# A residual encoder block on one core: the first weight chunk packed with x^T, three staggered chunks, later border transposes, and the last column quarter apart

## The chip, the cores and the metric

The kernel runs on one NeuronCore of one Trainium2 chip. The metric is the device time of one execution in microseconds (us); the runs shown are the median of three with the lowest and the highest. Engines are named as the profile names them: PE is TensorE (PEld its weight loads), DVE is VectorE, ACT is ScalarE, POOL is GpSimd and SP is SyncE, which here only issues DMAs.

## The reference

One layer on x of 256 tokens by 1024 features, all in float32 (D_FF = 2816):

```python
h = rmsnorm(x, ffn1_pre_g);  x = x + 0.5 * rmsnorm(swiglu(h, ffn1_w_in, ffn1_w_down), ffn1_post_g)
h = rmsnorm(x, mix_pre_g)
q_a, f_a, i_a, g_a, q_b, k_b, v_b, f_b, gates = split(h @ w_in)
o_a = rmsnorm(hgrn2_chunkwise(q_a, f_a, i_a), hg_norm_g) * silu(g_a)      # gated linear recurrence
o_b = fox_attention(q_b, k_b, v_b, f_b + fox_f_bias)                      # causal attention with decay
g = sigmoid(gates + b_gate)
y = g[:, 0] * (o_a @ w_branch_a) + g[:, 1] * (o_b @ w_branch_b)
x = x + rmsnorm(y @ w_out, mix_post_g)
x = x + rmsnorm(mem_cross_attention(rmsnorm(x), rmsnorm(mem), w_mq, w_mkv, w_mo), mem_post_g)
h = rmsnorm(x, ffn2_pre_g);  x = x + 0.5 * rmsnorm(swiglu(h, ffn2_w_in, ffn2_w_down), ffn2_post_g)
```

where swiglu(h) is (silu(gate) * up) @ w_down and rmsnorm divides by the root mean square of a row.

## The kernel before

**Arithmetic.** Each float32 product is made of three matmuls. An operand is split into a rounded part ("hi", made by ACT as a cast) and the remainder ("lo" or "lT", made by DVE as a subtraction), and PE adds hi·hi, hi·lo and lo·hi. Weights come in units of 128 x 1024 (512 KB). `unit` (L113) loads one into a buffer `raw` (4 of these), casts it to `hi` (L122, ACT) and makes `lo` (L123, DVE); there are 8 buffers each of `hi` and `lo`, so a further unit can be split only when PE has used up an older one. Activations are kept transposed, features on the partitions, in a `Pair` of hi and lo tiles with 8 blocks (kb) of 128 features. `proj_tok` multiplies one half of the tokens (h = 0 or 1, 128 each) by a chunk of four units: 24 matmuls of 512 columns, kb 0 to 7 in order.

**The head.** L397 to L411. x^T comes over the ACT queue in five DMAs, unit 0 over the SP queue in two halves and units 1 to 3 whole. PE makes 14 warm-up passes on a tile of ones (`WARM` = 7 matmuls). For each kb, `gain_split` (L242) writes hi = x·gain (L247 on ACT, for the very first block L245 on DVE) and the remainder (L248, DVE). `act_first` (L320) then does chunk 0 and chunk 1 of the first feed-forward for both halves: 2 x 48 matmuls into the four `acc` banks.

**A feed-forward.** `ffn` (L288) takes 11 chunks of 256 hidden columns. `act_tok` multiplies, `act_evac` (L306) applies Silu (L308, ACT) and the product (L310, DVE), `flush` (L294) transposes the result and splits it, and `down` (L333) adds the chunk's part of the output into `accs[h][n]`, one PSUM bank for each half h and each 512 columns n. The `down` of the last `STAG` = 4 chunks is kept to the end: first all of half 0, then all of half 1.

**A border.** When half 0 of a stage is summed, `post` (L272) makes the sandwich norm: Square with a row sum on ACT (`ssq`, L219), the product with the gain row on DVE (L279), an inverse root from small DVE operations on 128 x 1 (`rstd_of`, L200: a bit trick, then three Newton steps of two operations), and x += on DVE (L283). `half` (L426) then transposes the new x (`to_T`, L250: 8 transposes of 128 x 128 on PE, L256, into two PSUM banks, then 8 `gain_split`s) and takes the row sums of x. PE meanwhile works on half 1. `after(i)` (L83) places such work behind the i-th matmul from a mark: the constants `L_F1`, `L_IA`, `L_WO`, `L_MK`, `L_MO` say how many matmuls into the next piece of work the transposes come. The program's own scheduler orders each engine's instructions under these limits; the order is fixed when the program is built. There are three such borders: A, from the first feed-forward to the mixer's `i_a` projection; B, from `w_out` to the memory attention; C, from `mo` (the memory attention's output projection, 48 matmuls for half 0, then 48 for half 1) to the second feed-forward.

**The end.** `post(accs[1], 1, grow, 0.5, True)` (L393) makes the last half's norm, and two stores of 256 KB on the SP queue end the program.

Of the kernel before, what the change touches and what calls it, by code (L numbers as in the profile page):

```python
# [16 lines left out]
P = 128  # L17
# [5 lines left out]
NFF = D_FF // FC  # L23
EPS = 1e-6
BIG = 1e30
# [18 lines left out]

WARM = 7

X_AT = 6

# [16 lines left out]
@with_exitstack  # L65
def block_kernel(ctx: ExitStack, tc: tile.TileContext, wts, x_in, xT_in, mem_in, memT_in, cols, rows, fbias, masks, out):
    nc = tc.nc
# [44 lines left out]

    def unit(name, i, parts=1):  # L113
        u = _AT[name] + i
        if u not in cache:
            raw = wp.tile([P, D], F32, tag="raw", name=nm("raw"), bufs=4)
            hi = wp.tile([P, D], F32R, tag="hi", name=nm("hi"), bufs=8)
            lo = wp.tile([P, D], F32R, tag="lo", name=nm("lo"), bufs=8)
            for a in range(0, D, D // parts):
                cut = slice(a, a + D // parts)  # L120
                loads.append(nc.sync.dma_start(raw[:, cut], wts[u][:, cut]).ins)
                S.copy(hi[:, cut], raw[:, cut])  # L122
                V.tensor_tensor(out=lo[:, cut], in0=raw[:, cut], in1=hi[:, cut].bitcast(F32), op=ALU.subtract)  # L123
            cache[u] = (hi, lo)
        return cache[u]
# [74 lines left out]
    def rstd_of(s, scaled=True):  # L200

        v = s1(name="v")
        V.tensor_scalar(out=v, in0=s[:, 0:1], scalar1=s[:, 1:2], scalar2=D * EPS, op0=ALU.add, op1=ALU.add)
        y = s1(name="y")
        V.tensor_scalar(out=y.bitcast(I32), in0=v.bitcast(I32), scalar1=-0.5, scalar2=1597463007.0, op0=ALU.mult, op1=ALU.add)
        for c in (3.0, 12.0, 768.0):
            t = s1(name="t")
            V.scalar_tensor_tensor(out=t, in0=v, scalar=y, in1=y, op0=ALU.mult, op1=ALU.mult)  # L208
            y2 = s1(name="y")
            V.scalar_tensor_tensor(out=y2, in0=t, scalar=c, in1=y, op0=ALU.subtract, op1=ALU.mult)  # L210
            y = y2
        if not scaled:
            return y
        r = s1(name="rstd")
        V.tensor_scalar(out=r, in0=y, scalar1=-1.0 / 256.0, scalar2=None, op0=ALU.mult)
        return r
# [54 lines left out]

    def post(ps, h, grow, factor=1.0, last=False):  # L272

        s = s1(2, name="ss2")
        ts = []
        for j in range(2):
            ssq(s[:, j : j + 1], ps[j])
            t = sp.tile([P, 512], F32, tag="z2", name=nm("post"), bufs=3)
            V.scalar_tensor_tensor(out=t, in0=ps[j], scalar=-factor / 256.0, in1=grow[:, j * 512 : (j + 1) * 512], op0=ALU.mult, op1=ALU.mult)  # L279
            ts.append(t)  # L280
        r = rstd_of(s, scaled=False)
        for j, (t, xh) in enumerate(zip(ts, x_halves(h))):
            V.scalar_tensor_tensor(out=xh, in0=t, scalar=r, in1=xh, op0=ALU.mult, op1=ALU.add)  # L283
            if last:
                nc.sync.dma_start(out[h * P : (h + 1) * P, j * 512 : (j + 1) * 512], xh)


    def ffn(w_in, w_dn, X, r2, n_tok, i_row, first_half, second_half=None):  # L288
# [17 lines left out]
        def act_evac(ps, c, h):  # L306
            sg = sp.tile([P, FC], F32, tag="c1", name=nm("sg"), bufs=7)
            S.activation(sg, ps[:, :FC], AF.Silu, scale=r2[h])  # L308
            a = sp.tile([P, FC], F32, tag="c1", name=nm("at"), bufs=7)
# [22 lines left out]

        def down(c, h):  # L333
            act = acts[c]
            hs = slice(h * P, (h + 1) * P)
            for j in range(2):
                wh, wl = unit(w_dn, 2 * c + j)
                ah, al = act[:, 0, j, hs], act[:, 1, j, hs]
                for n in range(2):
                    ns = slice(n * 512, (n + 1) * 512)  # L340
                    for i, (a, w) in enumerate(((ah, wh), (ah, wl), (al, wh))):
                        MM(accs[h][n], a, w[:, ns], start=(c == 0 and j == 0 and i == 0), stop=(c == NFF - 1 and j == 1 and i == 2))

# [20 lines left out]
        for c in range(n_tok, NFF):  # L364
# [10 lines left out]
            while done < min(c - 1, NFF - STAG):  # L375
# [3 lines left out]
                flush(n + L_ACT)  # L379
                done += 1  # L380
        m = len(log)
# [5 lines left out]
        for c in range(NFF - STAG, NFF):  # L387
            down(c, 1)
        if first_half:
            first_half(m)  # L390
# [13 lines left out]
    S.activation(warm, ones[:, 0:1], AF.Silu)  # L404
    wps = trp()
    for _ in range(WARM):
        MM(wps[:, :P], ones, ones, start=True, stop=True)
    for j in range(4):
        unit("f1_in", j, 2 if j == 0 else 1)
        for i in range(2):  # L410
            gain_split(X1, 2 * j + i, xT[j][:, i, :T], xT[j][:, i, T:], first=2 * j + i == 0)  # L411

# [340 lines left out]
    def gates(c):  # L753
        u = chunk("gates", c)
        z = m4([P, 2, 512], n="zg")
        brow = sp.tile([P, 512], F32, tag="brow", name=nm("brow"), bufs=2)
        nc.sync.dma_start(brow, rows[4 + c // 2, c % 2 * 512 : c % 2 * 512 + 512].partition_broadcast(P))
        for h in range(2):
# [58 lines left out]

    def rows_proj(ps, X, name, h, kbs):
        a, b = h * P, h * P + P
        for kb in kbs:  # L820
            wh, wl = unit(name, kb)
            for n in range(2):
                ns = slice(n * 512, (n + 1) * 512)
# [22 lines left out]
    for c in range(2):  # L846
        u = chunk("mk", c)
        KM.more()
        for j in range(2):
# [97 lines left out]
def _layout(inputs):  # L947
# [41 lines left out]
    def col(v):  # L989
# [11 lines left out]
        [((s == t) if m == 0 else ((s // m) % 2 == 0) & (t // m == s // m + 1)).astype(np.int32) for m in LEVELS], axis=1  # L1001
    )
    r = {
        "wts": wts, "x": nat(a["x"]), "xT": np.concatenate([tra(a["x"]), col(a["ffn1_pre_g"][0])[:, :, None]], axis=2), "mem": nat(a["mem"]), "memT": tra(a["mem"]),
        "cols": cols, "rows": rows, "fbias": a["fox_f_bias"][0].reshape(8, 1), "masks": masks,
# [18 lines left out]
```

## Time and profile before

| what | value |
|---|---|
| runs shown | 808.42 us median of 3 (807.83 to 810.88) |
| the profiled execution | 807.36 us, of which the profile's span is 805.6 us |
| granted TensorE clock, mean | 0.997 |
| weight DMAs, SP queue | 260 whole units of 512 KB, 4.3 us from issue to landing (median) |
| GpSimd | 9.2 us busy |

The page gives the busy time of each engine and its costliest groups. Groups that a view prints by line look like "line engine operation out<-in shapes xcount | busy, mean ns of one | idle before, and what ended it". A timeline row is "start, length, engine, line, operation, tiles, count", with the idle time before it and what ended it in square brackets; rows of like instructions are merged, and the count says how many. Two matmuls of 512 columns start 0.227 us apart though each is shown with 0.39 us, since they are pipelined. The chain of waits follows the work that ended last back to the start.

### The profile page before, as it was taken

The page shows a single profiled execution, that of the slowest core. Times are in us where ns is not written, and L with a number is a line of the kernel's source. Part 1 is how long each engine was busy: PE and PEld are TensorE (multiplying, and loading weights), DVE is VectorE, ACT ScalarE, POOL GpSimd, SP SyncE. Part 2 cuts the span into 40 slices and gives each one's busy share as a digit, 9 for nine tenths or more (in the row PEclk, how much of TensorE's full clock was granted, in tenths as well). Part 3 has the DMA queues.
Part 4 walks back from the last instruction along what each step waited for, and adds up shares of the span by engine and source line. Part 5 has one row for each costly group of instructions (what it writes and reads, how often), then busy time and mean ns, then how long its engine had stood idle before and what let it go on. Part 6 is the DMA issues. An engine that isn't in the chain of part 4 may idle for free.

```text
span 805.6 us, 12769 instructions
## 1 busy us (share of the span) xinstructions
PE 792.6 (98%) x5040; PEld 679.4 (84%) x5040; DVE 525.1 (65%) x837; ACT 414.3 (51%) x623; POOL 9.2 (1%) x20
## 2 busy tenths in 40 slices
PE   8999999999999999999999999999999999999996
PEld 6888888888899889998888888999887788888884
DVE  6865545548776897678675666975659655545544
ACT  6754444537754435447674445645647654434531
POOL 0000000000000100200000000000000000000000
PEclk9999999999999999999999999999999999999998
DMA  8866654555455463643486555455425656665521
GB/s 331 302 223 209 211 200 157 193 173 183 164 203 171 171 195 123 212 155 120 139 291 235 177 161 201 146 197 196 151 77 186 210 185 206 209 201 166 182 79 52
DMA packets 41867, 147.90 MB, mean 184 GB/s; under 512 B 4808, under 2 KB 5200, under 8 KB 41808
## 3 DMA queue, kind: packets, MB, share of 16 engines
q1 hardware_dynamic: 40624, 144.46, 53.2%
q0 software_dynamic: 464, 1.58, 0.6%
q10 hardware_dynamic: 720, 1.05, 0.4%
q8 instruction: 39, 0.64, 0.3%
q14 instruction: 20, 0.16, 0.1%
HBM read 146.02 MB, written 1.06 MB: 183 GB/s over the span
## 4 chain that ended last, share of the span: by engine, by line
PE 89%; DVE 4%; DMA 2%; issue 2%; ACT 1%; SPq 0%; DVEq 0%; ACTq 0%
PE mm L80 63%; PE acc L80 23%; DMA raw<-in_wts_dram 2%; DVE lo L123 2%; PE tr L303 1%; PE tr L80 1%; ACT junk L219 1%; DVE xs L283 1%; PE tr L256 1%; DVE t L208 1%; DVE y L210 0%; ACT hi L122 0%; PE tr L712 0%; DVE post L279 0%; PE tr L901 0%
## 5 line engine op out<-in xcount | busy, mean ns | idle before, releaser
L123 DVE TENSOR_TENSOR lo<-raw,hi 128x1024 fp32r<-128x1024 f32 (+1 forms) x262 | 317.7, 1222 | 93.3 <-ACT hi L122 83.7
L122 ACT CAST hi<-raw 128x1024 fp32r<-128x1024 f32 (+1 forms) x262 | 270.8, 1047 | 140.0 <-PE mm L80 105.1
L80 PE MATMUL mm<-lo,hT 128*128 128x512 f32 x576 | 225.9, 392 | 0.0
L80 PE MATMUL mm<-hi,hT 128*128 128x512 f32 x576 | 225.6, 392 | 0.0
L80 PE MATMUL mm<-hi,lT 128*128 128x512 f32 x576 | 225.1, 391 | 0.1
L80 PEld LDWEIGHTS mm<-hi,lT 128*128 128x128 f32 x576 | 108.2, 188 | 23.0 <-DVE lT L248 0.8
L80 PEld LDWEIGHTS mm<-hi,hT 128*128 128x128 f32 x576 | 108.2, 188 | 22.6 <-ACT hT L247 0.5
L80 PEld LDWEIGHTS mm<-lo,hT 128*128 128x128 f32 x576 | 108.2, 188 | 21.7
L80 PE MATMUL acc<-hi,act 128*128 128x512 f32 x352 | 111.8, 391 | 0.0
L80 PE MATMUL mm<-hT,lo 128*128 128x256 f32 x392 | 111.3, 284 | 0.0
L80 PE MATMUL mm<-hT,hi 128*128 128x256 f32 x392 | 111.2, 284 | 0.0
L80 PE MATMUL mm<-lT,hi 128*128 128x256 f32 x392 | 111.1, 283 | 0.0
L80 PEld LDWEIGHTS acc<-hi,act 128*128 128x128 f32 x352 | 66.1, 188 | 13.4
L80 PEld LDWEIGHTS mm<-lT,hi 128*128 128x128 f32 x392 | 75.2, 192 | 0.1
L80 PEld LDWEIGHTS mm<-hT,hi 128*128 128x128 f32 x392 | 75.2, 192 | 0.1
L80 PEld LDWEIGHTS mm<-hT,lo 128*128 128x128 f32 x392 | 75.2, 192 | 0.1
L80 PE MATMUL acc<-lo,act 128*128 128x512 f32 x176 | 70.0, 398 | 0.0
L308 ACT ACTIVATE sg<-mm,rstd 128x256 f32<-128x256 f32 x40 | 19.0, 474 | 76.2 <-PE mm L80 76.2
L310 DVE SCALAR_TENSOR_TENSOR at<-mm,rstd,sg 128x256 f32<-128x256 f32 x40 | 19.2, 480 | 58.8 <-ACT sg L308 58.8
L80 PEld LDWEIGHTS acc<-lo,act 128*128 128x128 f32 x176 | 33.1, 188 | 6.4
L80 PE MATMUL acc<-hi,hT 128*128 128x512 f32 x96 | 35.5, 396 | 1.6 <-ACT hi L122 1.1
L80 PE MATMUL acc<-hi,lT 128*128 128x512 f32 x96 | 35.4, 396 | 0.5 <-DVE lT L248 0.5
(175 smaller groups left out, 630.2 us busy)
## 6 DMA issues: line engine op xcount, KB each, us to landing
raw<-in_wts_dram SPq DMA_DIRECT2D x260, 512.0 KB, 4.3
grow<-in_rows_dram SPq DMA_DIRECT2D x4, 512.0 KB, 5.8
brow<-in_rows_dram SPq DMA_DIRECT2D x4, 256.0 KB, 4.9
xs<-in_x_dram SPq DMA_DIRECT2D x2, 512.0 KB, 5.5
cbm<-cd POOLq DMA_DIRECT2D x2, 512.0 KB, 8.5
memT<-in_memT_dram SPq DMA_DIRECT2D x2, 512.0 KB, 7.5
ms<-in_mem_dram SPq DMA_DIRECT2D x2, 512.0 KB, 7.8
out_dram<-xs SPq DMA_DIRECT2D x4, 256.0 KB, 2.1
```

What stands on the lines that cost most here:

```text
L80: log.append(PE.matmul(*args, **kw).ins)
L122: S.copy(hi[:, cut], raw[:, cut])
L123: V.tensor_tensor(out=lo[:, cut], in0=raw[:, cut], in1=hi[:, cut].bitcast(F32), op=ALU.subtract)
L208: V.scalar_tensor_tensor(out=t, in0=v, scalar=y, in1=y, op0=ALU.mult, op1=ALU.mult)
L219: S.activation(junk[:, : src.shape[-1]], src, AF.Square, accum_out=dst)
L256: PE.transpose(ps[:, j * P : (j + 1) * P], src(kb), ident)
L283: V.scalar_tensor_tensor(out=xh, in0=t, scalar=r, in1=xh, op0=ALU.mult, op1=ALU.add)
L303: PE.transpose(trv[:, j, h * P : (h + 1) * P], ats[c, h][:, j * P : (j + 1) * P], ident)
L308: S.activation(sg, ps[:, :FC], AF.Silu, scale=r2[h])
L310: V.scalar_tensor_tensor(out=a, in0=ps[:, FC:], scalar=r2[h], in1=sg, op0=ALU.mult, op1=ALU.mult)
```

## The change

The diff below is cut; the new numeric constants `SC_RSTD`, 16.0 and 40/3 only carry scale factors of the new polynomial.

- **Head.** The host packs, for each kb, x^T's block, the matching 512 columns of chunk 0's weights and the gains into one row of 776 floats. Eight DMAs on the SP queue bring them; x^T's own five DMAs on the ACT queue and units 0 to 3 disappear. `X_AT`, the weight load behind which x itself is fetched, goes from 6 to 10, `WARM` from 7 to 8. The gate rows (`brow`) are held behind the latest weight load.
- **Staggered chunks.** `STAG` goes from 4 to 3. For half 0, and for half 1 of the second feed-forward, the kept `down`s go through the left 512 columns of all three chunks before the right 512.
- **Borders.** `L_F1` 18 to 24, `L_IA` 22 to 36, `L_WO` 18 to 12 and `L_MK` 46 to 84 with both transposes of border B moved into the `mk` projection, `L_MO` 18 to 21. `mo` does kb 0 to 2 for both halves first, then kb 3 to 7 of half 0 (left, then right columns), then kb 3 to 7 of half 1.
- **Inverse root.** Two Newton steps are replaced by one and a fourth-order step: five operations where there were six.
- **The end.** The last chunk's right columns of half 1 are done as two quarters of 256, and `post_last` treats left, third and fourth quarter apart, takes the root with Sqrt on ACT, and stores in three parts on two queues. A Sqrt on a dummy behind the last Silu precedes it.

```diff
-STAG = 4
-L_ACT = 15
-L_F1 = 18
-L_IA = 22
-L_WO = 18
-L_MK = 46
-L_MO = 18
+STAG = 3
+L_ACT = 21
+L_F1 = 24
+L_IA = 36
+L_WO = 12
+L_MK = 84
+L_MO = 21
-WARM = 7
-X_AT = 6
+WARM = 8
+X_AT = 10
...
+    def parts_of():
+        return [wp.tile([P, D], F32R, tag=t, name=nm(t), bufs=8) for t in ("hi", "lo")]
...
-        for c in (3.0, 12.0, 768.0):
-            t = s1(name="t")
-            V.scalar_tensor_tensor(out=t, in0=v, scalar=y, in1=y, op0=ALU.mult, op1=ALU.mult)
-            y2 = s1(name="y")
-            V.scalar_tensor_tensor(out=y2, in0=t, scalar=c, in1=y, op0=ALU.subtract, op1=ALU.mult)
-            y = y2
+        V.scalar_tensor_tensor(out=t, in0=v, scalar=y, in1=y, op0=ALU.mult, op1=ALU.mult)
+        V.scalar_tensor_tensor(out=z, in0=t, scalar=3.0, in1=y, op0=ALU.subtract, op1=ALU.mult)
+        V.scalar_tensor_tensor(out=t, in0=v, scalar=z, in1=z, op0=ALU.mult, op1=ALU.mult)
+        V.scalar_tensor_tensor(out=w, in0=t, scalar=40.0 / 3.0, in1=t, op0=ALU.subtract, op1=ALU.mult)
+        V.scalar_tensor_tensor(out=y, in0=w, scalar=80.0, in1=z, op0=ALU.add, op1=ALU.mult)
...
+    def post_last(ps, h, grow, factor):
+        cuts = [(0, 0, 512), (1, 0, 256), (1, 256, 512)]
+        for i, (j, a, b) in enumerate(cuts):
+            ssq(s[:, i : i + 1], ps[j][:, a:b])
+            if i == 1:
+                V.tensor_scalar(out=sums, in0=s[:, 0:1], scalar1=s[:, 1:2], scalar2=D * EPS, op0=ALU.add, op1=ALU.add)
+            if i == 2:
+                S.activation(y, s[:, 2:3], AF.Sqrt, bias=sums)
+                V.tensor_tensor(out=v, in0=s[:, 2:3], in1=sums, op=ALU.add)
+            V.scalar_tensor_tensor(out=t, in0=ps[j][:, a:b], scalar=scaled, in1=grow[:, j * 512 + a : j * 512 + b], op0=ALU.mult, op1=ALU.mult)
+        V.reciprocal(z, y)
+        V.scalar_tensor_tensor(out=t, in0=v, scalar=z, in1=z, op0=ALU.mult, op1=ALU.mult)
+        V.scalar_tensor_tensor(out=r, in0=t, scalar=3.0, in1=z, op0=ALU.subtract, op1=ALU.mult)
+        for t, (j, a, b), eng in zip(ts, cuts, (nc.sync, nc.scalar, nc.sync)):
+            V.scalar_tensor_tensor(out=xh, in0=t, scalar=r, in1=xh, op0=ALU.mult, op1=ALU.add)
+            eng.dma_start(out[h * P : (h + 1) * P, j * 512 + a : j * 512 + b], xh)
...
+            if c == NFF - 1 and h == 1 and not first_half:
+                with tc.issue_after(silu.ins):
+                    S.activation(warm, ones[:, 0:1], AF.Sqrt)
...
-        for c in range(NFF - STAG, NFF):
-            down(c, 0)
+        for cut in (left, right):
+            for c in range(NFF - STAG, NFF):
+                down(c, 0, (cut,))
...
-            post(accs[1], 1, grow, 0.5, True)
+            for cut in (left, right):
+                for c in range(NFF - STAG, NFF):
+                    if (c, cut) != (NFF - 1, right):
+                        down(c, 1, (cut,))
+            for cut in ((512, 768), (768, 1024)):
+                down(NFF - 1, 1, (cut,))
+            post_last(accs[1], 1, grow, 0.5)
...
-    xT = [m4([P, 2, T + 1], n="xT") for _ in range(KB // 2)]
-    for kb in range(2):
-        S.dma_start(xT[0][:, kb], xT_in[:, kb])
-    for j in range(1, 4):
-        S.dma_start(xT[j], xT_in[:, 2 * j : 2 * j + 2])
+    heads = [m4([P, T + 512 + KB], n="head") for _ in range(KB)]
+    for kb in range(KB):
+        loads.append(nc.sync.dma_start(heads[kb], head_in[kb]).ins)
...
+    for kb in range(KB):
+        if kb % 2 == 0:
+            cache[_AT["f1_in"] + kb // 2] = parts_of()
+        hi, lo = (p[:, kb % 2 * 512 : kb % 2 * 512 + 512] for p in cache[_AT["f1_in"] + kb // 2])
+        w = heads[kb][:, T : T + 512]
+        S.copy(hi, w)
+        gain_split(X1, kb, heads[kb][:, :T], heads[kb][:, T + 512 + kb : T + 512 + kb + 1], first=kb == 0)
+        V.tensor_tensor(out=lo, in0=w, in1=hi.bitcast(F32), op=ALU.subtract)
...
-    half(X3, r3, 0, G_MEM, m + L_WO)
...
-        if c == 0:
-            half(X3, r3, 1, G_MEM, m + L_MK)
+            if c == 0:
+                half(X3, r3, j, G_MEM, m + (L_WO, L_MK)[j])
...
-    for h in range(2):
-        m = len(log)
-        rows_proj(po[h], AO, "mo", h, range(0, 4))
-        rows_proj(po[h], AO, "mo", h, range(4, 8))
-        if h == 1:
-            half(X4, r4, 0, G_F2, m + L_MO)
-        post(po[h], h, g3)
+    for kb in range(3):
+        for h in range(2):
+            rows_proj(po[h], AO, "mo", h, (kb,))
+    for n in range(2):
+        rows_proj(po[0], AO, "mo", 0, range(3, KB), (n,))
+    post(po[0], 0, g3)
+    m = len(log)
+    rows_proj(po[1], AO, "mo", 1, range(3, KB))
+    half(X4, r4, 0, G_F2, m + L_MO)
+    post(po[1], 1, g3)
```

More of the change, by code (lines that the diff above doesn't have):

```diff
@@ L116, in unit @@
             raw = wp.tile([P, D], F32, tag="raw", name=nm("raw"), bufs=4)
[L117 to L123, printed above, removed]
+            hi, lo = parts_of()
+            loads.append(nc.sync.dma_start(raw, wts[u - 4]).ins)
+            S.copy(hi, raw)
+            V.tensor_tensor(out=lo, in0=raw, in1=hi.bitcast(F32), op=ALU.subtract)
             cache[u] = (hi, lo)
@@ L270, in load_row, with post @@
         return r
-    def post(ps, h, grow, factor=1.0, last=False):
+    def post(ps, h, grow, factor=1.0, store=False):
         s = s1(2, name="ss2")
@@ L338, in down @@
                 ah, al = act[:, 0, j, hs], act[:, 1, j, hs]
[L339 to L340 removed]
+                for lo, up in cols:
                     for i, (a, w) in enumerate(((ah, wh), (ah, wl), (al, wh))):
[L342 removed]
+                        MM(accs[h][lo // 512][:, lo % 512 : lo % 512 + up - lo], a, w[:, lo:up], start=(c == 0 and j == 0 and i == 0), stop=(c == NFF - 1 and j == 1 and i == 2 and up % 512 == 0))
         for c in range(n_tok):
@@ L386, in ffn @@
         m = len(log)
-        for c in range(NFF - STAG, NFF):
-            down(c, 1)
         if first_half:
+            for c in range(NFF - STAG, NFF):
+                down(c, 1)
             first_half(m)
@@ L756, in gates @@
         brow = sp.tile([P, 512], F32, tag="brow", name=nm("brow"), bufs=2)
-        nc.sync.dma_start(brow, rows[4 + c // 2, c % 2 * 512 : c % 2 * 512 + 512].partition_broadcast(P))
+        with tc.issue_after(loads[-1]):
+            nc.sync.dma_start(brow, rows[4 + c // 2, c % 2 * 512 : c % 2 * 512 + 512].partition_broadcast(P))
         for h in range(2):
@@ L821, in rows_proj @@
             wh, wl = unit(name, kb)
-            for n in range(2):
+            for n in cols:
                 ns = slice(n * 512, (n + 1) * 512)
@@ L1002, in _layout @@
     )
+    xT = tra(a["x"])
+    gain = col(a["ffn1_pre_g"][0])
+    head = np.stack(
+        [np.concatenate([xT[:, kb], wts[kb // 2][:, kb % 2 * 512 : kb % 2 * 512 + 512], gain], axis=1) for kb in range(KB)]
+    )
     r = {
-        "wts": wts, "x": nat(a["x"]), "xT": np.concatenate([tra(a["x"]), col(a["ffn1_pre_g"][0])[:, :, None]], axis=2), "mem": nat(a["mem"]), "memT": tra(a["mem"]),
+        "wts": wts[4:], "head": head, "x": nat(a["x"]), "mem": nat(a["mem"]), "memT": tra(a["mem"]),
         "cols": cols, "rows": rows, "fbias": a["fox_f_bias"][0].reshape(8, 1), "masks": masks,
```

40 lines of the change are left out of this document (28 added, 12 removed).

## The prediction

> **What bounds the kernel now.** I read the page first, then the chain of waits, then the timeline at the places where the chain leaves PE.
>
> ```profile
> span 805.6 us, 12769 instructions
> PE 792.6 (98%) x5040; PEld 679.4 (84%) x5040; DVE 525.1 (65%) x837; ACT 414.3 (51%) x623; POOL 9.2 (1%) x20
> PE 89%; DVE 4%; DMA 2%; issue 2%; ACT 1%; SPq 0%; DVEq 0%; ACTq 0%
> 10.73 19.03 PE acc L80 x82
> 47.53 10.88 PE mm L80 x48
> 516.46 13.55 PE mm L80 x113
> ```
>
> PE sets the time. The change removes no matmul, so it can move only the stretches without PE: the head, the borders and the tail. A 512-column matmul costs 10.88/48 = 0.227 us, a 256-column one 13.55/113 = 0.12.
>
> **Head.** The timeline of the first 8 us, and two stretches of the windows view (length, busy time and count of PE, PEld, DVE, ACT, POOL, clock, DMA share, GB/s), with one row of the DMA issues:
>
> ```profile
> 3.43 1.28 ACT L404 ACT_TABLE_LOAD   x1 [3.43 <-issue]
> 4.68 0.35 DVE L245 TENSOR_SCALAR hT<-xT 128x256 fp32r<-128x256 f32 x1 [3.66 <-DMA xT<-in_xT_dram]
> 4.73 0.20 ACT L404 ACTIVATE warm<-ones 128x1 f32<-128x1 f32 x1
> 4.84 0.60 ACT L122 CAST hi<-raw 128x512 fp32r<-128x512 f32 x1
> 5.07 0.48 DVE L248 SCALAR_TENSOR_TENSOR lT<-xT,hT 128x256 fp32r<-128x256 f32 x1
> 5.47 0.69 DVE L123 TENSOR_TENSOR lo<-raw,hi 128x512 fp32r<-128x512 f32 x1
> 5.49 0.72 PE L80 MATMUL acc<-hi,hT 128*128 128x512 f32 x2 [1.07 <-ACT hi L122]
> 6.56 0.51 ACT L247 ACTIVATE hT<-xT 128x256 fp32r<-128x256 f32 x1
> 0.00:6.00 6.00, 3.86 (x16) 3.53 (x17) 1.45 (x4) 2.00 (x3) 0.71 (x6) 1.00 0.58 172
> 6.00:11.00 5.00, 4.05 (x14) 2.12 (x14) 3.20 (x6) 3.06 (x6) 0.00 (x0) 1.00 1.04 412
> xT<-in_xT_dram ACTq DMA_DIRECT2D x2, 128.5 KB, 3.9
> ```
>
> The first two chunks are 96 matmuls, 21.76 us at 0.227. They begin at 5.49 and end with the row of 82, at 29.76, so 2.51 us are lost after the start. At that start 128.5 KB of x^T and 256 KB of weights, 384.5 KB together, had come over two queues, x^T by 4.68 and the weights by 4.84. The new first block is 128 x 776 x 4 bytes = 388 KB on one queue: I take 4.7. ACT has issued no DMAs by then, so its table load (1.28) and the warming activation are long over, and the cast of 0.60 ends at 5.3, where PE starts. Each later block costs DMA 397,312 bytes / 412 GB/s = 0.96 us, ACT 0.60 + 0.51 = 1.11, DVE 0.48 + 0.69 = 1.17 and PE 6 x 0.227 = 1.36. PE is the slowest of the four, so after a wait at the second block and refilling (I allow 0.45) it runs on: 5.3 + 21.76 + 0.45 = 27.5, **-2.3 us**. Bounds: with a start at 5.0 and no wait -3.0; if the queue keeps the 172 GB/s of the first 6 us, +4.5 (a rival below). The eight issues on SP replace its five; ACT loses its five; x is fetched behind eleven loads instead of seven, but its norm is due only when chunk 2 needs the `acc` banks, after 29.76. The gate rows, needed mid-kernel, now wait for a weight load; the 24 matmuls (5.4 us) ahead of their first use hide that.
>
> **Borders.** What is removed first; a group of the lines view, two of the waits view, and rows of borders A and C:
>
> ```profile
> L256 PE MATMUL tr<-ident,xs 128*128 128x128 f32 x48 | 7.4, 280 | 1.4 <-DVE xs L283 1.2 <-issue 0.2
> PE tr L303 <- DVE at L310: 0.7, 1, 0.7
> PEld acc L80 <- ACT hT L136: 0.5, 1, 0.5
> 188.22 0.63 PE L256 MATMUL tr<-ident,xs 128*128 128x128 f32 x4 [0.20 <-issue]
> 194.20 0.39 PE L80 MATMUL mm<-hi,hT 128*128 128x512 f32 x1
> 195.84 0.61 DVE L248 SCALAR_TENSOR_TENSOR lT<-tr,cols_s,hT 128x128 fp32r<-128x128 f32 x2 [0.80 <-ACT hT L247]
> 203.92 1.32 PE L256 MATMUL tr<-ident,xs 128*128 128x128 f32 x8 [0.72 <-DVE xs L283]
> 208.34 0.61 DVE L248 SCALAR_TENSOR_TENSOR lT<-tr,cols_s,hT 128x128 fp32r<-128x128 f32 x2
> 601.90 1.23 DVE L123 TENSOR_TENSOR lo<-raw,hi 128x1024 fp32r<-128x1024 f32 x1
> 603.94 0.63 PE L256 MATMUL tr<-ident,xs 128*128 128x128 f32 x4 [0.25 <-DVE xs L283]
> 606.90 0.60 DVE L248 SCALAR_TENSOR_TENSOR lT<-tr,cols_s,hT 128x128 fp32r<-128x128 f32 x2
> 608.97 0.60 DVE L248 SCALAR_TENSOR_TENSOR lT<-tr,cols_s,hT 128x128 fp32r<-128x128 f32 x2
> 609.88 0.39 PE L80 MATMUL mm<-hi,hT 128*128 128x512 f32 x1
> 611.34 0.61 DVE L248 SCALAR_TENSOR_TENSOR lT<-tr,cols_s,hT 128x128 fp32r<-128x128 f32 x2 [0.32 <-ACT hT L247]
> ```
>
> PE waits 1.4 us for border transposes, 0.7 once for an activation's transposes (placed 6 matmuls, 1.36 us, later by `L_ACT` 21) and 0.5 for the attention output ahead of `mo`, of which I count 0.4 because PE overlaps a little. All can go: **-2.5**.
>
> What is added: with three staggered chunks the cover at A, half 1's `down`s, shrinks from 48 to 36 matmuls; at C, half 1's part of `mo` shrinks from 48 to 30. The next projection starts 12 x 0.227 = 2.7 and 18 x 0.227 = 4.1 us earlier against the split that it reads: 191.5 and 605.8 in the old times. Block kb's remainder is due 0.68 kb + 0.45 after that start. The rows of two are blocks (4, 1), (5, 2) and (6, 3), an order I infer from the two banks taking turns. Kept at the old pace, C's blocks 1, 2, 3 are ready at 607.5, 609.6, 611.9 and due at 606.9, 607.6, 608.3: each wait pushes the next, 3.7 in all (the last: 611.9 - 608.3). At A, 196.4 - 194.0 = 2.5. That is the upper bound at the old pace. The lower is the split of half 1 at A, which meets no weight split: its block 3 is done 5.0 us after its transposes (208.95 against 203.92). At that pace C, with its transposes at 603.94, waits 0.6 (608.9 - 608.3) and A, with its at 188.22, nothing. I choose A 0.4 and C 1.3, nearer the lower end: at C three of the next eight units are split before half 0 ends, at A two, so a weight split of 1.23 leaves the stretch; and the root is one operation shorter, which puts the x update close ahead of the second weight split (601.90). Together **+1.7**. Border B's transposes go into `mk`, which reads the memory and not x, so the move costs nothing there; if `mk` did read x, PE would wait there as it does at A and C. The Sqrt's table load (1.28) sits on ACT behind the last Silu, while PE does 12 `down` matmuls (2.7) before it needs ACT's next cast; with no such cover it would cost up to 1.28.
>
> **Tail.** From the last matmul on:
>
> ```profile
> 797.59 0.39 PE L80 MATMUL acc<-hi,act 128*128 128x512 f32 x1
> 798.12 0.60 ACT L219 ACTIVATE junk<-acc 128x512 f32<-128x512 f32 x1
> 798.61 0.19 ACT L219 ACTIVATION_READ_ACCUMULATOR junk<-acc 128x1 f32 x1
> 801.02 0.16 DVE L210 SCALAR_TENSOR_TENSOR y<-t,y 128x1 f32<-128x1 f32 x1
> 801.22 1.42 DVE L283 SCALAR_TENSOR_TENSOR xs<-post,y,xs 128x512 f32<-128x512 f32 x2
> L308 ACT ACTIVATE sg<-mm,rstd 128x256 f32<-128x256 f32 x40 | 19.0, 474 | 76.2 <-PE mm L80 76.2
> L310 DVE SCALAR_TENSOR_TENSOR at<-mm,rstd,sg 128x256 f32<-128x256 f32 x40 | 19.2, 480 | 58.8 <-ACT sg L308 58.8
> 188.88 0.37 ACT L247 ACTIVATE hT<-tr,cols_s 128x128 fp32r<-128x128 f32 x1 [0.23 <-PE tr L256]
> L247 ACT ACTIVATE hT<-tr,cols_s 128x128 fp32r<-128x128 f32 x64 | 20.9, 364 | 4.6 <-DVE lT L248 3.2 <-PE tr L256 1.1
> ```
>
> From Square to the finished root takes 801.18 - 798.12 = 3.06 us. Whether the third quarter's Square can run under the fourth quarter's matmuls turns on the last two rows. The four transposes of one bank run from 188.22 to 188.85, and ACT, which wants only the first, starts at 188.88. L247 also waits 3.2 us in all for L248, though it only reads another part of the same bank. So accesses to one bank take turns, PE, ACT and DVE alike, and I take turns for the quarters: Square 0.47 + the rest of the read (0.1), product 0.48, Square 0.57, Sqrt 0.2 (the warming row), three operations of about 0.2, and gaps of 0.04 to 0.1: 2.6, that is -0.46. Three updates of x for two cost +0.1, twelve short matmuls for six +0.08, and the last store is half as large, about -0.1: **-0.4**. Bounds: -1.5 with the third quarter hidden (its Square and product, 1.1, gone), +0.9 if the Sqrt's table came only here.
>
> [...]
>
> **The sum.** -2.3 - 2.5 + 1.7 - 0.4 = -3.5 us against the profiled execution, 807.36 to 803.9. The median shown lies 1.06 above that execution; on its footing I forecast 808.42 - 3.5 = **804.9 us**. Its own range is 803.4 to 807.
>
> **The rivals.**
>
> 1. The shorter covers suffice: no new wait. For it: half 1's split at A shows the pace without weight splits; against it, at least five units are still to be split at both borders. -5.2: 803.2.
> 2. The third quarter does hide under the fourth. Against it stand the two rows of turns. -1.1 more: 803.8.
> 3. Slower: the cover at A and C is too short by so much that half 1's norm falls into half 0's split. Both borders keep the old pace (2.5 + 3.7), and the split waits besides for two Squares with their reads (2 x 0.79) or two products (2 x 0.69), about 1.5 at each: 9.2 in place of 1.7. -5.2 + 9.2 = +4.0: 812.4. It decides against the change once the new waits exceed 5.2. For it: the old rows themselves; against it: fewer weight splits.
> 4. The head change doesn't do what it says: the queue delivers a block in 397,312 / 172 GB/s = 2.3 us. The eighth lands at 20.9, its cast, scaling and matmuls end at 23.4, chunk 1 at 34.2, +4.5: 808.42 + 4.5 - 1.2 = 811.7. It turns against the change from 1.67 us a block. The 412 GB/s of the next window speak against it.
>
> **Chances.** Forecast 0.45, rival 1 0.33, rival 2 0.07, rival 3 0.12, rival 4 0.03. Half a per cent is 4.0 us, about what a measurement here can tell from no change. Faster than 804.4 are 0.3 of the forecast's cases, 0.85 of rival 1's and 0.6 of rival 2's: 0.45. Slower than 812.5 are under half of rival 3's and a few of rival 4's: 0.06. The rest, 0.49, lies between. The range runs from 801.5 (rival 1 with a better head) to 809.5.
>
> **What would show it.** The first real matmul near 5.3 and no gap over 0.4 after the second block; the row of chunks 0 and 1 ending near 27.5. At A and C, PE idle ahead of the projection's kb 1 to 3, ended by L248 (or by nothing, rival 1; by L248 behind L219 and L279, rival 3). No idle ahead of L256 or L303. In the tail, the third quarter's Square after the last matmul's start, and the end about 7.6 us after it instead of 8.0. A gap in the middle of a feed-forward, where I expect none, would upset the sum.

## The result, and the profile after

The changed kernel takes 811.06 us (median of 20 runs, 809.91 to 813.09), the kernel before 808.32 us in the same session (20 runs, 807.28 to 810.88). The ratio is 1.0035, with a 95% interval of 1.0028 to 1.0043: slower by 2.7 us, where 3.5 us of gain were forecast.

The profiled execution of after took 812.8 us with a span of 811.0. It lies 1.74 above its median, and the one of before 0.96 below its own; so the two profiles differ by 5.4 us, the medians by 2.7. The profiles show where the time sits, the runs how much of it there is on average.

The row of busy times on the page of after (busy us, share of the span, count):

```profile
PE 793.5 (98%) x5048; PEld 682.7 (84%) x5048; DVE 521.0 (64%) x820; ACT 416.8 (51%) x631; POOL 8.8 (1%) x20
```

One piece of its chain of waits (start us, us, what):

```profile
11.32 24.25 PE acc L81 x96
```

PE is busy 0.9 us longer than before in a span 5.4 us longer; most of the rest is idle time. The 96 matmuls of chunks 0 and 1 begin at 11.32 instead of 5.49 and end at 35.57 instead of 29.76: 5.81 us, more than the whole difference of the two profiles. What PE waited for at 11.32 stands in the timeline of after:

```profile
3.79 0.62 ACT L457 CAST hi<-head 128x512 fp32r<-128x512 f32 x1 [1.54 <-DMA head<-in_head_dram]
4.44 0.69 DVE L459 TENSOR_TENSOR lo<-head,hi 128x512 fp32r<-128x512 f32 x1 [3.42 <-ACT hi L457]
5.08 0.62 ACT L457 CAST hi<-head 128x512 fp32r<-128x512 f32 x1 [0.68 <-DMA head<-in_head_dram]
...
7.59 0.62 ACT L457 CAST hi<-head 128x512 fp32r<-128x512 f32 x1 [1.89 <-DMA head<-in_head_dram]
...
9.57 0.62 ACT L457 CAST hi<-head 128x512 fp32r<-128x512 f32 x1 [0.37 <-DMA head<-in_head_dram]
10.10 1.70 ACT L252 ACTIVATE hT<-head 128x256 fp32r<-128x256 f32 x4
10.22 0.69 DVE L459 TENSOR_TENSOR lo<-head,hi 128x512 fp32r<-128x512 f32 x1 [0.30 <-ACT hi L457]
10.83 0.35 DVE L250 TENSOR_SCALAR hT<-head 128x256 fp32r<-128x256 f32 x1
...
11.32 1.19 PE L81 MATMUL acc<-hi,hT 128*128 128x512 f32 x2 [6.48 <-DVE hT L250]
...
12.31 1.06 PE L81 MATMUL acc<-hi,lT 128*128 128x512 f32 x2
...
14.02 1.05 PE L81 MATMUL acc<-hi,hT 128*128 128x512 f32 x2
...
16.33 0.63 PE L81 MATMUL acc<-hi,hT 128*128 128x512 f32 x2
...
16.80 0.62 PE L81 MATMUL acc<-hi,lT 128*128 128x512 f32 x2
```

Block 0 was there at 3.79, when its cast began, and DVE's scaling of it (L250) needs only that block. Yet in DVE's own order it stands behind five weight remainders (L459), each of which waits for ACT's cast of the same block, and the fifth cast waits for block 4, which landed at 9.57. ACT's order has the same fault: five casts, then four scalings in a row (10.10). Both engines took their instructions here in the order that was fixed when the program was built, so work that was ready at 3.8 stood until 10.83, behind a transfer that it does not use.

The last rows show a second loss. From 12.31 to 14.02 four matmuls start, 0.43 us each; from 16.33 to 16.80 two, 0.235 each. PE began at half rate. The windows view (length, busy time and count of PE, PEld, DVE, ACT, POOL, clock, DMA share, GB/s) has a granted clock of 1.00 there, so that column does not show it; the counts do, 10 matmul starts against 20 in stretches of equal length:

```profile
11.30:15.70 4.40, 4.38 (x10) 3.42 (x11) 4.40 (x11) 4.40 (x10) 0.00 (x0) 1.00 1.02 410
16.00:20.40 4.40, 4.40 (x20) 3.62 (x20) 4.40 (x5) 3.89 (x7) 0.00 (x0) 1.00 1.03 394
```

Of what PE and its weight loads waited for, four rows of the waits view of after (us in total, times, longest):

```profile
PE acc L81 <- DVE hT L250: 6.5, 1, 6.5
PE tr L846 <- DVE zg L864: 1.3, 1, 1.3
...
PEld acc L81 <- ACT hT L137: 0.6, 1, 0.6
...
PEld mm L81 <- DVE lT L253: 0.5, 2, 0.3
```

and two groups of its lines view:

```profile
L261 PE MATMUL tr<-ident,xs 128*128 128x128 f32 x48 | 6.6, 275 | 0.6 <-DVE lT L253 0.4 <-DVE xs L288 0.2
L338 PE MATMUL tr<-ident,at 128*128 128x128 f32 x88 | 14.2, 274 | 0.6 <-DVE at L348 0.6
```

The border transposes (L256 before, L261 now) wait 0.6 us instead of 1.4. Of that, 0.2 is for the update of x (1.2 before), and 0.4 for a remainder (L253) is a new wait, at border B. The activation's transposes (L303, now L338) wait 0.6 instead of 0.7. In the projections weight loads wait 0.5 us in all for the remainder L253 and 0.5 for the scaling L252, together 1.0 against 1.3 before, so the new waits at borders A and C are small. `mo` waits 0.6 for the attention output (0.5 before). The 1.3 at L846 is new: in the branch stage a weight unit came late.

The end, from the last matmul:

```profile
803.44 0.28 PE L81 MATMUL acc<-hi,act 128*128 128x256 f32 x1
803.82 0.38 ACT L224 ACTIVATE junk<-acc 128x256 f32<-128x256 f32 x1 [3.46 <-PE acc L81]
...
804.45 0.41 DVE L309 SCALAR_TENSOR_TENSOR post<-acc,grow 128x256 f32<-128x256 f32 x1
804.96 0.38 ACT L224 ACTIVATE junk<-acc 128x256 f32<-128x256 f32 x1 [0.67 <-DVE post L309]
...
805.47 0.29 ACT L305 ACTIVATE y<-ss,v 128x1 f32<-128x1 f32 x1
```

The third quarter's Square starts at 803.82, only after PE's last matmul (803.44 and 0.28 long), and the fourth's, at 804.96, waits for the third's product (804.45 and 0.41 long): ACT, DVE and PE take turns here. The root's Sqrt, 0.29 us at 805.47, needs no table load: ACT's last one, 1.28 us, stands at 787.41 ahead of the dummy. From the start of the last matmul to the end it is 811.0 - 803.44 = 7.56 us against 8.01 before.

### The profile page after: what moved, and what is told of

Same layout as the page of the kernel before. It is cut to its first block, busy times and chain, and to the rows that moved or that the text cites. A ratio compares the mean times of both kernels' runs of the same rounds, so it can differ in the third digit from the quotient of the medians.

```text
span 811.0 us, 12778 instructions
## 1 busy us (share of the span) xinstructions
PE 793.5 (98%) x5048; PEld 682.7 (84%) x5048; DVE 521.0 (64%) x820; ACT 416.8 (51%) x631; POOL 8.8 (1%) x20
## 4 chain that ended last, share of the span: by engine, by line
PE 92%; DVE 2%; DMA 2%; ACT 2%; issue 1%; SPq 0%; DVEq 0%; ACTq 0%
PE mm L81 62%; PE acc L81 26%; DMA raw<-in_wts_dram 1%; PE tr L338 1%; PE tr L81 1%; DMA head<-in_head_dram 1%; PE tr L261 1%; DVE lo L124 1%; ACT junk L224 1%; ACT hi L123 1%; PE tr L760 0%; PE tr L846 0%; PE tr L949 0%; SPq L446 0%; DVE lT L253 0%
## 5 line engine op out<-in xcount | busy, mean ns | idle before, releaser
L124 DVE TENSOR_TENSOR lo<-raw,hi 128x1024 fp32r<-128x1024 f32 x257 | 312.4, 1226 | 127.2 <-ACT hi L123 118.7
L123 ACT CAST hi<-raw 128x1024 fp32r<-128x1024 f32 x257 | 266.0, 1051 | 170.6 <-PE mm L81 101.9
L81 PE MATMUL acc<-hi,act 128*128 128x512 f32 (+1 forms) x356 | 112.5, 389 | 0.0
L81 PE MATMUL acc<-lo,act 128*128 128x512 f32 (+1 forms) x178 | 70.3, 395 | 0.0
```

Of the source, the lines that this page charges most:

```text
L81: log.append(PE.matmul(*args, **kw).ins)
L123: S.copy(hi, raw)
L124: V.tensor_tensor(out=lo, in0=raw, in1=hi.bitcast(F32), op=ALU.subtract)
```

## The experiments

The first theory was: the loss sits in the head, and there in the order of ACT's and DVE's instructions, not in the transfers. Its rivals were the pace of eight transfers on one queue, and the borders. All ratios below are to the kernel before, run beside each kernel on the same chip, with 95% intervals; they are formed from all runs of both kernels and not from the medians of the table.

| kernel | median us | ratio to before |
|---|---|---|
| after | 811.06 | 1.0035 (1.0028 to 1.0043) |
| after, old head | 806.69 | 0.9972 (0.9962 to 0.9982) |
| before, new head | 814.20 | 1.0063 (1.0050 to 1.0076) |
| after, order forced | 804.76 | 0.9946 (0.9934 to 0.9957) |
| the same once more | 803.91 | 0.9945 (0.9927 to 0.9962) |
| after, two queues | 805.25 | 0.9961 (0.9950 to 0.9973) |
| after, 38 warm-up matmuls | 809.20 | 1.0003 (0.9994 to 1.0013) |
| before, ordered head alone | 807.09 | 0.9978 (0.9965 to 0.9991) |

**Old head in the changed kernel.** The head, `unit`, `WARM` and `X_AT` as before, with the host's packing; all else as changed.

> The changed kernel with the head of before (x^T and the weights as separate transfers, 7 warm-up matmuls); three staggered chunks, deeper border work and the last quarter stay. Theory (the loss sits in the head: block 0's scalings stand behind the casts of blocks 0 to 4, first matmul 11.32 instead of 5.49): chunk 0+1 ends at 29.8 us again and the time falls by 5 to 5.8 us from 811.06, to 805.3 to 806.1. Rival (the borders or the tail are what costs, the head's delay is absorbed): the time stays over 808.5, although the first matmul is back at 5.5.

Measured 806.69 us, 0.9972; chunks 0 and 1 end at 29.84. The ratio fell by 0.0063, 5.1 us. The head is what makes the change slow, and the rest of it is a gain of about 2.3 us (0.0028). The median lies 0.6 us above the expected range; the fall by the ratio is within the 5 to 5.8 us that were expected.

**New head alone.** The opposite: the kernel before, with the new head only.

> The kernel before with only the new head (eight blocks on one queue, 8 warm-up matmuls). Theory: first matmul near 11.3, chunk 0+1 ends near 35.5, 5 to 5.8 us above before's 808.3: 813.3 to 814.1. Rival (borders or tail cost): not over 809.

814.20 us, 0.1 above the expected range, 1.0063; first matmul at 10.60. The two answers multiply to the whole: 1.0063 x 0.9972 = 1.0035. So the head and the rest add up.

**Order forced, same queue.** Each block's cast is tied behind the previous block's scaling on ACT, and on DVE scaling, x^T's remainder and the weight remainder of a block come in that order.

```diff
+    seen = [None, None]
     for kb in range(KB):
...
-        S.copy(hi, w)
-        gain_split(X1, kb, heads[kb][:, :T], ..., first=kb == 0)
-        V.tensor_tensor(out=lo, in0=w, in1=hi.bitcast(F32), op=ALU.subtract)
+        with ExitStack() as es:
+            for q in seen:
+                if q is not None:
+                    es.enter_context(tc.issue_after(q))
+            c = S.copy(hi, w)
...
+        seen = [(q if kb else c).ins, l.ins]
```

> The changed kernel, same eight transfers on the same queue, but on ScalarE the cast of block k+1 is tied behind the scaling of block k, and on VectorE each block's products behind the ones of the block before. Theory (it is the order, not the queue): first matmul at 4.3 to 5, which takes away 6.3 to 7 us of the late start and with it the 2 us of half-rate matmuls after the long idle time, less 1 to 2 us of waits for blocks 2 and later, which land 1 us apart: 802.5 to 805. Rival (the blocks' pace on one queue sets the start): first matmul and time unchanged, 810 or more. Second rival (only lateness counts, the half rate stays): 805 to 806.

804.76 us, 0.9946. The timeline of this kernel, and one piece of its chain:

```profile
3.75 0.62 ACT L463 CAST hi<-head 128x512 fp32r<-128x512 f32 x1 [1.50 <-DMA head<-in_head_dram]
3.75 0.35 DVE L465 TENSOR_SCALAR hT<-head 128x256 fp32r<-128x256 f32 x1 [2.73 <-DMA head<-in_head_dram]
...
4.42 0.73 PE L81 MATMUL acc<-hi,hT 128*128 128x512 f32 x2
```

```profile
4.50 22.30 PE acc L81 x96
```

The same eight transfers on the same queue now feed PE from 4.42 on, and chunks 0 and 1 end at 26.80 instead of 35.57. (A part of this difference between two profiles is not the order: block 2 came 1.4 us after block 1 here and 2.5 in the profile of after.) From 1.0035 to 0.9946 it is 0.0089, 7.2 us for the order of some thirty instructions. The rival of the pace falls, and this version is 4.4 us faster than before (0.0054); none of the others is faster by more than the intervals.

**Two queues.** One line: the odd blocks are issued by ACT instead of SP.

```diff
-        loads.append(nc.sync.dma_start(heads[kb], head_in[kb]).ins)
+        loads.append((nc.sync if kb % 2 == 0 else nc.scalar).dma_start(heads[kb], head_in[kb]).ins)
```

> The changed kernel with the eight blocks issued in turns from SP's and ScalarE's queue; its instructions then come out block by block too, with VectorE's weight difference of block 0 ahead of its two scalings. Theory (order): within 1 us of the run with the order forced on one queue, first matmul 0.3 to 0.7 us later than there: 803 to 805.5. Rival (pace of one queue): blocks land clearly less than 1 us apart and this run is over 1.5 us faster than the one with the order forced on one queue.

805.25 us, 0.9961: within the expected distance of the forced order, and no faster. The first matmul, however, came 2.2 us later than there in the profile below, not 0.3 to 0.7 (this execution took 808.10 us, 2.9 above its median). With the transfers issued so, the order comes out block by block without being forced. Why eight transfers on one queue bring the other order is not settled. Its timeline:

```profile
6.14 0.35 DVE L250 TENSOR_SCALAR hT<-head 128x256 fp32r<-128x256 f32 x1
...
6.63 1.19 PE L81 MATMUL acc<-hi,hT 128*128 128x512 f32 x2 [1.78 <-DVE hT L250]
...
7.62 1.05 PE L81 MATMUL acc<-hi,lT 128*128 128x512 f32 x2
...
8.47 1.05 PE L81 MATMUL acc<-lo,hT 128*128 128x512 f32 x2
```

In this profiled execution PE started at 6.63 and again at half rate (two matmuls in the 0.85 us from 7.62 to 8.47).

**Long warm-up.** `WARM` 8 to 38, nothing else.

> The changed kernel with 38 instead of 8 warm-up matmuls on ones, nothing else: PE is kept busy until about 10.8 us, the first block's scalings stand where they stood. Theory (of the head's loss, some 2 us are 11 matmul intervals at 0.427 instead of 0.227 us after the idle 6.5 us): first matmul still near 11, its intervals 0.23 us from the start, 2 us less: 808.5 to 809.5. Rival (the half rate has nothing to do with what PE did before): intervals of 0.427 us again and 811 us.

809.20 us, 1.0003. The ratio falls by 0.0032, 2.6 us, although the first matmul comes at 12.22, 0.9 later than in the profile of after, since the warm-up ran on. Its rows:

```profile
8.73 3.74 PE L81 MATMUL tr<-ones 128*128 128x128 f32 x32
12.22 0.70 PE L81 MATMUL acc<-hi,hT 128*128 128x512 f32 x2
12.77 0.63 PE L81 MATMUL acc<-hi,lT 128*128 128x512 f32 x2
13.23 0.62 PE L81 MATMUL acc<-lo,hT 128*128 128x512 f32 x2
```

Two matmuls take 0.46 from 12.77 on, and the late warm-up passes 0.117 each (3.74 / 32), where the 16 of after took 3.78, 0.24 each. So here the half rate depends on what PE did before, and 2.6 of the 7.2 us between this head and the ordered one are won back by a longer warm-up alone.

**The tail undone.** With the forced order; one norm over the last half, no early square root.

```diff
-            for cut in (left, right):
...
-            post_last(accs[1], 1, grow, 0.5)
+            for c in range(NFF - STAG, NFF):
+                down(c, 1)
+            post(accs[1], 1, grow, 0.5, True)
```

> The kernel with the forced order, its tail as before: last chunk's second half in one piece, one norm over both halves, no square root ahead. Theory: the new tail is worth the 0.45 us that the profiles show from the last matmul to the end (8.01 against 7.55): 804.76 plus 0.45, 805.2. Rival (the third quarter really hides): 806 or more. Second rival (the tail gives nothing): 804.8 or less.

804.84 us, 0.9950 (0.9937 to 0.9963), against 0.9946. The difference of 0.3 us has an interval of about 1.4 us to either side, so the runs can't tell 0.4 from nothing, and only just leave 1.5. Against 1.5 stand the rows of the tail, in which the engines take turns.

**The borders undone.** With the forced order; `STAG`, all delays, the place of the norms' halves and the order of `mo` as before.

> The kernel with the forced order, with four staggered chunks, the delays, the place of the norms' halves and the order of the mo products as before; head and tail stay new. Theory (borders now give about 1.7 us: 2.1 measured for borders and tail together, less 0.45 of the tail): 806.1 to 806.7. Rival of the prediction (new waits at the borders eat most of it): 804.8 to 805.6.

803.93 us, 0.9941 (0.9928 to 0.9955). Neither the theory nor the rival: undoing the deeper placement costs nothing that the runs resolve. Yet the rest beside the head is worth 2.3 us, so something else must take the place of the deeper placement.

**The gates' bias rows early.** With the forced order; without the tie behind the last weight transfer.

```diff
-        with tc.issue_after(loads[-1]):
-            nc.sync.dma_start(brow, rows[4 + c // 2, ...
+        nc.sync.dma_start(brow, rows[4 + c // 2, ...
```

> The kernel with the forced order, its bias rows of the gates no longer tied behind the last weight transfer. Theory (the wait of 1.0 to 1.5 us for a weight unit near 460 us comes from the pace of transfers after a pause, not from that tie): 804.76 within 0.5, the wait still there in the profile. Rival (the tie makes it): wait gone, 803.7.

804.60 us, 0.9947 (0.9930 to 0.9963), and the wait in the branch stage is still there:

```profile
456.86 1.05 ACT L123 CAST hi<-raw 128x1024 fp32r<-128x1024 f32 x1 [2.90 <-DMA raw<-in_wts_dram]
459.92 0.63 PE L859 MATMUL tr<-ident,zg 128*128 128x128 f32 x4 [1.06 <-DVE zg L877]
```

The tie does not make it. A PE gap of 0.9 to 1.9 us stands there in eight of the fourteen profiles with the new head and in none of the three with the old one; what decides when that unit lands stays open.

**What the rest consists of.** Three kernels beside a second run of the forced order.

> The kernel with the forced order once more, on the chip and beside the runs of before of this call, as the base of the next three: ratio to before 0.995 within 0.001, 804.8 us; with the run before of the same kernel it says how far two calls differ.

803.91 us, 0.9945 (0.9927 to 0.9962): the ratios of the two sessions agree to 0.0001, which is closer than their intervals warrant.

> The kernel before with only the new head, in the forced order (8 warm-up matmuls): borders, tail, norms as before. Theory (the parts add up; old head beside all other edits was 2.1 us faster than before): the base plus 2.1, 806.9. Rival (the ordered head gives all of it, the rest nothing): 804.8.

807.09 us, 0.9978 (0.9965 to 0.9991). The theory: the ordered head is worth 1.8 us, the rest comes on top of it.

> The kernel with the forced order, borders as before (four staggered chunks, delays, places of the norms' halves, mo order), and also the last chunks of half 0 in whole rows, not left columns first. Theory (the earlier first norm of half 0 had kept what the borders give): base plus 0.5 to 1.2 us, 805.3 to 806. Rival (borders and columns give nothing): the base within 0.4.

805.34 us, 0.9956 (0.9942 to 0.9969). The time fits the theory, but the profile contradicts its reason: the border transposes wait 0.4 us, less than the 0.9 with the columns apart. The two ratios, 0.9956 and 0.9941, are not resolved either.

> The changed kernel with the head and the borders of before; norms' arithmetic, left columns first, the gates' bias rows and the tail stay new. Theory (borders are worth about 1 us, as the profiles' gaps say): 807.5 to 808. Rival 1 (borders worth nothing, as the run with borders undone said): 806.7, as the old head with the new borders. Rival 2 (borders are all of the 2.1 us): 808.8, the time of before.

806.54 us, 0.9971 (0.9961 to 0.9982): rival 1. Old or new borders, with the old head 0.9971 and 0.9972. The waits of the border transposes, by the lines view of the ordered head alone, and of borders and columns undone (the old head with old borders has this second line word for word):

```profile
L256 PE MATMUL tr<-ident,xs 128*128 128x128 f32 x48 | 7.4, 280 | 1.4 <-DVE xs L283 1.2 <-issue 0.2
```

```profile
L261 PE MATMUL tr<-ident,xs 128*128 128x128 f32 x48 | 7.2, 277 | 0.4
```

The two kernels with this second line have the old placement and wait only 0.4. What they have and the first has not: the shorter root, the tail, the bias rows. The tail comes after all borders, so the root was suspected.

**Root and placement apart.** The new root is one Newton step and one fourth-order step where the old has three Newton steps. All three with the ordered head: the kernel before with the new root; the changed kernel with the old root; and the latter with the old borders too.

```diff
-        for c in (3.0, 12.0, 768.0):
...
+        V.scalar_tensor_tensor(out=w, in0=t, scalar=40.0 / 3.0, in1=t, op0=ALU.subtract, op1=ALU.mult)
+        y = s1(name="y")
+        V.scalar_tensor_tensor(out=y, in0=w, scalar=80.0, in1=z, op0=ALU.add, op1=ALU.mult)
```

> The kernel before with the ordered head and the new reciprocal root (one operation less in each norm), nothing else. Theory (the shorter root is what takes the border waits away: with borders undone they stayed at 0.4 us, with the ordered head alone they are 1.4): border transposes wait 0.4 us in the lines view, time 1 to 2 us under the ordered head alone's 807.1: 805 to 806. Rival (columns, tail or bias rows did it): waits 1.4 us, 807.

> The kernel with the forced order and all new borders, with the root of before (one operation more). Theory (deeper placement hides the waits by itself too, so root and placement replace each other): border waits under 0.8 us, time within 0.7 of 804.4. Rival (only the root hides them): waits of 1.2 us or more, 805.5 to 806.5.

> The kernel with the forced order, with both the borders and the root of before; left columns first, bias rows and tail stay new. Theory (either one hides the waits, here neither is there): border waits back at 1.2 to 1.4 us, 805.5 to 806.5. Rival (left columns first or the tail give the 2 us of the rest): waits 0.4 us, 804 to 804.8.

| root | borders | border transposes wait | ratio to before |
|---|---|---|---|
| old | old (ordered head alone) | 1.4 us | 0.9978 |
| old | old (with tail and columns new) | 1.5 us | 0.9977 (0.9963 to 0.9990) |
| new | old (ordered head, new root) | 0.4 us | 0.9964 (0.9948 to 0.9980) |
| new | old (borders undone, tail and columns new) | 0.9 us | 0.9941 (0.9928 to 0.9955) |
| old | new | 0.6 us | 0.9958 (0.9943 to 0.9974) |
| new | new (forced order) | 0.6 us | 0.9946 (0.9934 to 0.9957) |

The medians of the three new kernels are 805.81, 805.24 and 807.22 us. The first and its waits came as expected; the second lies 0.1 us beyond the expected distance, the third 0.7 above its range. Their waits, 0.6 and 1.5, bear the theory out (under 0.8, and 1.2 to 1.4, were expected).

The lines view of these three kernels in their order, and then of borders undone:

```profile
L261 PE MATMUL tr<-ident,xs 128*128 128x128 f32 x48 | 7.3, 277 | 0.4
```

```profile
L257 PE MATMUL tr<-ident,xs 128*128 128x128 f32 x48 | 6.7, 275 | 0.6 <-DVE xs L284 0.2 <-issue 0.2
```

```profile
L257 PE MATMUL tr<-ident,xs 128*128 128x128 f32 x48 | 7.4, 280 | 1.5 <-DVE xs L284 1.3 <-issue 0.2
```

```profile
L261 PE MATMUL tr<-ident,xs 128*128 128x128 f32 x48 | 7.3, 278 | 0.9 <-DVE xs L288 0.5
```

Either one takes most of the waits away, and both together take them away once. That is why undoing the placement alone cost nothing. The second, fourth, fifth and sixth row differ in nothing but root and borders; all four have tail and columns new. There the intervals of "neither" (0.9963 to 0.9990) and of "both" (0.9934 to 0.9957) lie apart, as do those of "neither" and of the new root alone (0.9928 to 0.9955). So the runs resolve that the pair is worth something, 0.0031 or 2.5 us (1.1 to 3.9), about the whole gain beside the head, and the shorter root alone gives it too. For the deeper placement alone (0.9958) the intervals overlap, and so they do for the new root without the new tail and columns (0.9964 against 0.9978).

How can one small operation do that? DVE's timeline at border C, of the ordered head alone and of the same kernel with the short root, which differ in nothing but the root:

```profile
598.80 0.20 DVE L203 TENSOR_SCALAR v<-ss 128x1 f32<-128x1 f32 x1
...
600.01 1.22 DVE L123 TENSOR_TENSOR lo<-raw,hi 128x1024 fp32r<-128x1024 f32 x1
...
601.48 1.23 DVE L123 TENSOR_TENSOR lo<-raw,hi 128x1024 fp32r<-128x1024 f32 x1
602.62 1.41 DVE L283 SCALAR_TENSOR_TENSOR xs<-post,y,xs 128x512 f32<-128x512 f32 x2
```

```profile
598.10 0.20 DVE L204 TENSOR_SCALAR v<-ss 128x1 f32<-128x1 f32 x1
...
599.30 1.22 DVE L124 TENSOR_TENSOR lo<-raw,hi 128x1024 fp32r<-128x1024 f32 x1
...
600.63 1.42 DVE L288 SCALAR_TENSOR_TENSOR xs<-post,y,xs 128x512 f32<-128x512 f32 x2
```

From the sum to the update of x it is 3.82 us with the old root and 2.53 with the new. Of the 1.29 between them about 0.2 is the missing operation; the rest is a weight remainder. With one operation fewer, the order that was fixed when the program was built has the update ahead of the second remainder instead of behind it. It is so for half 0 at all three borders in these two kernels, and likewise in the kernel before (two remainders) and with borders undone (one). At half 1 of border A, where PE waited longest (0.74 with the old root, not at all with the new), the update follows the sum after 1.93 us against 1.65; DVE also reaches the sum 1.3 us later, counted from the projection's first matmul. That this delay is left over from half 0 is likely, but not tested.

## Why the prediction was wrong

- **The head, -2.3 forecast, +5.1 measured (1.0063).** The step that failed: "the cast of 0.60 ends at 5.3, where PE starts", and after it "it runs on". It took for granted that ACT and DVE work block by block, as the loop is written. The cast did end at 4.41, and block 0 had landed at 3.8, earlier than the 4.7 taken. But its scaling stood behind the casts and remainders of blocks 0 to 4, and the first matmul came at 11.32. The later blocks landed 1.0 to 1.3 us apart (0.96 forecast), with one pause of 2.5 before block 2.
- **The rate of the first matmuls.** "96 matmuls, 21.76 us at 0.227" had no term for a slow start. The chunk took 24.25 us in after, 2.5 more, most of it half rate: the first 12 matmuls needed 5.01 us (11.32 to 16.33), 2.3 more than at 0.227. With the order forced it took 22.30.
- **The head's price holds once its order does.** With the order that the prediction assumed, the head gives 0.9978, -1.8 us (-0.7 to -2.8), and the chunks end at 26.80 where 27.5 was forecast. The whole then stands at 804.76 us beside the forecast of 804.9, but this agreement is in part luck: against the kernel before it is -4.4 us where -3.5 was forecast, with a head that gave about 0.5 less and a rest that gave about 1.1 more.
- **Border waits removed, -2.5.** The transposes' 1.4 fell by 0.8, but the credit went to the placement alone. The shorter root takes the wait away as well, and the prediction named it only against the new wait at C. There it had the mechanism right, "the x update close ahead of the second weight split", and didn't see that this alone shortens the waits to be removed. The 0.7 of the activation's transposes stayed at 0.6 though they were placed six matmuls later, and `mo` waits as before.
- **New waits at A and C, +1.7.** The projections' weight loads wait 1.0 us for the split of x in the profile of after, less than the 1.3 before. The split keeps up; rival 1 was nearly right here, and rival 3 fell. At border B, where the move into `mk` was priced at nothing, PE waits 0.4. So the rest was forecast at -2.5 + 1.7 - 0.4 = -1.2 and gave -2.3.
- **Tail, -0.4.** In the profiles 8.01 became 7.56, -0.45, and the rows show turns, as taken (803.82 and 804.96, above); rival 2 fell. The last store, 128 KB, landed 2.0 us after its issue where those of 256 KB took 2.1 before, the 0.1 that was taken. The runs can't confirm so small a figure.
- **Rival 4** named the right place and nearly the right time (811.7), by luck: the reason was not a slow queue but the order behind it. Its 1.67 us a block is also only where the head alone breaks even; with the -1.2 of the rest the change would turn at 1.84.
- A gap where none was expected, at the branch stage (1.3 us in the profile of after), upset the sum as the prediction said it would. The bias rows are not its cause; what is stays open.

## What to carry to other kernels

When transfers are cut into blocks, look at the order in which the consuming engines take them before pricing the transfers: here an engine held by a late block held what was ready behind it, from 3.8 to 10.83 us, and a few ties between neighbours (7.2 us) were worth more than all other edits together (2.3). A term "PE starts when X is done" needs the place of X in its engine's order, and the rate at which PE starts, here 0.43 us a matmul instead of 0.227. A small operation is worth what its removal lets pass in a fixed order, here an update ahead of a weight remainder of 1.2 us. Two edits that remove the same wait must be priced together, and undone together, or each seems to be worth nothing.

## What was not expected of the hardware

PE ran at half rate after a start in the profile of after: 0.43 us against 0.227 for a 512-column matmul, and 0.24 for a warm-up pass against 0.117 late in the long warm-up, under a granted clock of 1.00 each time. With the tail undone, the real matmuls followed the warm-up with no idle time between, and yet:

```profile
1.07 3.78 PE L81 MATMUL tr<-ones 128*128 128x128 f32 x16 [1.07 <-DVE ones L187]
4.63 1.22 PE L81 MATMUL acc<-hi,hT 128*128 128x512 f32 x2
5.64 1.06 PE L81 MATMUL acc<-hi,lT 128*128 128x512 f32 x2
6.50 0.81 PE L81 MATMUL acc<-lo,hT 128*128 128x512 f32 x2
7.14 0.62 PE L81 MATMUL acc<-hi,hT 128*128 128x512 f32 x2
```

There PE still needed 0.43 us a matmul from 5.64 to 6.50 and came to full rate near 6.9, 5.8 us after its first pass; with the forced order its first two matmuls took 0.57 us (4.42 to 4.99) and the next ones started 0.23 apart, so it was at full rate 3.9 us after its first pass at the latest. What ends the half rate, and after how much work, no run here shows. The first six matmuls took 2.51 us with the tail undone (4.63 to 7.14) and 1.50 with the forced order (4.42 to 5.92). Such a difference can be a part of why executions of one kernel differ, 809.91 to 813.09 us for after; this is an estimate from these two profiles, and no run here shows how large a part.
